# A hybrid encoder trunk on one Trainium2 core: softmax weights are transposed undivided, and each head pair's output is divided by the sums afterwards

## The chip, the cores and the metric

The kernel runs on one core of one Trainium2 chip. The metric is the device time of one launch in microseconds (us), and less is better. The core has a matrix engine (TensorE, PE in the profile, with its weight loads shown apart as PEld), a vector engine (VectorE, DVE), an activation engine (ScalarE, ACT), a general engine (GpSimd, POOL) and a queue for transfers (SyncE, SP). Each takes its own instructions in the order in which the built program lists them, and waits where a semaphore tells it to.

## What is computed

Two layers, each with a Fourier group and an attention group side by side, then a convolutional feed-forward part:

```python
for l in range(DEPTH):                              # 2
    h = rmsnorm(x, norm1[l]);  p = h @ w_in[l]      # x: 512 x 1024
    y_f = fourier_mix(u, w_fourier[l], b_fourier[l])   # 512 columns
    q, k = rope(rmsnorm(q)), rope(rmsnorm(k))       # 8 heads of q, 2 of k and v
    y_a = windowed_gqa(q, k, v, sink[l])            # |i - j| <= 128
    x = x + concat(rmsnorm(y_f), rmsnorm(y_a)) @ w_o[l]
    h = rmsnorm(x, norm2[l])
    x = x + (silu(gate) * val) @ w_down[l]          # gate, val = dwconv3(h @ w_up)
```

In `windowed_gqa` a softmax runs over a query's masked scores and one more logit, the head's learned sink; the sink's weight is then dropped, so it only adds to the sum that the other weights are divided by:

```python
probs = softmax(concat([scores, sink_col], axis=-1), axis=-1)[..., :-1]
out = einsum("bnkgqj,bnjkd->bnqkgd", probs, vb)
```

## The kernel before

Activations are kept transposed: channels on the 128 partitions, the 512 positions along the free axis, in four blocks of 128. Each float32 product runs as three passes over operands that are split into a high and a low part (`mm3`, L102 to L107; `split`, L93 to L100: ACT writes the high part, DVE subtracts to get the low one). The whole program is unrolled. A list scheduler with a timeline model orders the instructions of each engine when the program is built, starting from the order in which the code issues them. Tiles come from pools with a fixed number of buffers to a tag: the tag `tF` has 6 buffers of 128x512, `tA` has 6, and in PSUM `tp` has 2 banks, `sc` 2, `av` 1 and `mm` 3 (L70 to L72).

One layer runs in these stages: norm statistics and q, k, v products (L266 to L286); folding of h for the Fourier half (L289 to L300); `prep`, `turn_q` and `turn_k`, which normalise, rotate, split and transpose q and k (L312 to L368); the first Fourier products (L426 to L442); attention by head pairs (`attention`, L376 to L416, called for pair 3 and then 0, 1, 2); two Fourier stages (L466 to L497); the Fourier group's own output product, in four column tiles j (L501 to L529), its norm and split (L530 to L536); the output projection `proj` (L541 to L549) first for the Fourier half (`ys`, 32 groups of three matmuls) and then for the attention half (`ya`, 32 groups); then the feed-forward part (L569 to L626), which takes most of the time.

Attention works on 32 pieces to a layer (8 heads, 4 query blocks each), here called blocks. For one block: two score matmuls into an `sc` bank (L390); DVE adds the mask and takes the row's smallest negated score against the sink, `nmax` (L394); ACT takes the exponential in place over the scores and one column more, which POOL had filled with the negated sink (L393), so that the accumulated sum `den` has the sink in it (L397); DVE inverts it (L398); POOL multiplies the weights by it (L399); PE transposes two or three 128x128 tiles into a `tp` bank (L402); ACT and DVE split them into `pT` (L405). After four blocks, the products with the values go to `py` in the one `av` bank (L412). After two heads, `py` is split with the gain (L415) and its square added to `accA` (L416).

Two things set the order around the change. `steps` collects the last transpose of each block (L403), and the matmuls of the Fourier half of the projection may not be issued on PE before the block `STEP0 + n` with `STEP0 = 12` (L546), so that they can stand between the blocks of the later pairs. And the Fourier tiles j take their evicted product `u`, their output `y` and, from j = 1, a square from the tag `tF` (L522, L524, L528), as do several other steps, but not `attention`.

Of the kernel before, what the change touches and what calls it, by code (L numbers as in the profile page):

```python
# [8 lines left out]
F32 = mybir.dt.float32  # L9
# [7 lines left out]
P = 128  # L17
# [20 lines left out]
def encoder_kernel(tc, t):  # L38
    """Residual stream kept transposed (channels on partitions, positions free).

    Every float32 product runs as three float32r passes over exact splits
    a = hi + lo:  hi*hi + lo*hi + hi*lo.  RMSNorm's per-position factor is
    applied after the product it precedes where that is possible, its gain before.
    """
# [24 lines left out]
    # ---------------------------------------------------------------- helpers  # L69
# [23 lines left out]
    def split(hi, lo, src, scale=None, eng=None):  # L93
        """hi + lo = src * scale; hi has float32r's mantissa, lo the rest."""
# [7 lines left out]
    def mm3(out, a, b, start, stop, after=None, **kw):  # L102
        """out (+)= a^T b over split operands a = (hi, lo), b = (hi, lo)."""
# [28 lines left out]
    def rsqrt(ssq, n, inv, tag, bufs=2):  # L132
        """(ssq * inv + EPS) ** -0.5 on [P, n]: bit estimate and Newton steps."""
# [11 lines left out]
    def col_rstd(acc, inv, tag="tp"):  # L145
        """rstd per position as columns [position in block, block]."""
# [5 lines left out]
    def row_rstd(r, tag="tp"):  # L152
        """The same factors along the free axis, on every partition."""
# [7 lines left out]
    # -------------------------------------------------------------- constants  # L161
# [27 lines left out]
    # first use of the activation tables and of the tensor engine while the inputs arrive  # L189
# [33 lines left out]
    # ---------------------------------------------------------- norm of x tile  # L223
# [8 lines left out]
    def norm_tile(k, g, acc):  # L232
        """Split x[k] * gain and add x[k]^2 to acc."""
# [8 lines left out]
    def fold(dst, src, eng):  # L242
        """src[..., 512] -> 0..256 even part, 257..511 odd part of 1..255."""
# [4 lines left out]
    def load_wu(l, kk):  # L248
        """Two row tiles of W_in's Fourier columns, folded."""
# [14 lines left out]
    for l in range(L):  # L264
        # ----------------------------------------- norm statistics, q, k, v
# [22 lines left out]
        # -------------------------------------- folded h for the Fourier half  # L288
# [13 lines left out]
        # ------------------- QK-norm, RoPE, transposed split q (pairs) and k  # L302
# [9 lines left out]
        def prep(us):  # L312
            """Normalised, rotated and split rows of the units us (head pairs, or "k")."""
# [34 lines left out]
        def turn_q(qs, tag):  # L348
            """[hi; lo] of the pair's two heads, transposed."""
# [23 lines left out]
        steps = []  # L373
        ya = {}

        def attention(p, first_pair):  # L376
            g = p // 2
            py = psum("av")
            first = True
# [335 lines left out]
```

## Time and profile before

| | before |
|---|---|
| median of 3 runs | 1119.74 us (1118.82 to 1119.9) |
| span of the profiled execution, first to last instruction | 1114.8 us |
| median less span (launch and end, outside the span) | 4.9 us |
| PE busy | 1067.8 us, 96% of the span |
| DVE, ACT, POOL busy | 789.6, 523.5 and 329.5 us |
| mean granted TensorE clock | 0.986 of full speed |

A time of the profiled execution other than its span is not listed, so the span stands for it, and the 4.9 us beside it is taken as fixed. In the profile's rows a group is a line, an engine, an operation and its tiles, with a count, busy time and mean duration; in the timeline a row is a start, a duration and how many instructions were merged. A matmul's row lasts longer than the distance to the next one, since matmuls are pipelined: PE can be shown busy while its stream has gaps. A float32 matmul (L156) is counted as two instructions.

### The profile page before, as it was taken

What the parts mean: (1) busy time and instruction counts of PE and PEld (TensorE: products, weight loads), DVE (VectorE), ACT (ScalarE), POOL (GpSimd) and SP (SyncE); (2) the same over time, 40 slices, a digit from 0 to 9 for tenths busy, and PEclk for the clock granted to TensorE, in tenths of its full rate; (3) what the DMA queues carried; (4) which work ended last, traced back from release to release, by engine and by line L of the source; (5) the groups of instructions that cost most, each with busy time, mean ns of one, the idle gap of its engine ahead of it and who ended that gap; (6) DMA issues with size and microseconds to landing.
All of it is one profiled execution on the core that took longest, in us unless ns stands there. A gap on an engine that the chain in (4) does not pass through costs nothing.

```text
span 1114.8 us, 14505 instructions
## 1 busy us (share of the span) xinstructions
PE 1067.8 (96%) x5187; PEld 894.0 (80%) x5187; DVE 789.6 (71%) x1362; ACT 523.5 (47%) x964; POOL 329.5 (30%) x370
## 2 busy tenths in 40 slices
PE   7878899999999999999997999999999999999998
PEld 6767788788888888888896878878888888888887
DVE  8998874888773377785549978477887535787732
ACT  4537763465442244543434677445554323554421
POOL 5778655311010001024207865561111000010100
PEclk9979999999999999999999999999999999999999
DMA  6312112223323323224321310223332322323241
GB/s 218 109 57 95 39 39 76 91 85 95 108 78 92 114 95 95 95 83 135 114 85 59 94 39 1 76 61 109 95 95 83 104 94 98 105 88 110 78 129 59
DMA packets 33226, 99.66 MB, mean 89 GB/s; under 512 B 3705, under 2 KB 8066, under 8 KB 33154
## 3 DMA queue, kind: packets, MB, share of 16 engines
q1 hardware_dynamic: 33154, 98.74, 28.1%
q8 instruction: 41, 0.67, 0.2%
q14 instruction: 31, 0.25, 0.1%
HBM read 96.63 MB, written 2.10 MB: 89 GB/s over the span
## 4 chain that ended last, share of the span: by engine, by line
PE 79%; DVE 14%; issue 2%; POOL 2%; ACT 1%; DMA 1%; SPq 0%; DVEq 0%; POOLq 0%; ACTq 0%
PE ps L107 25%; PE ps L105 25%; PE ps L106 25%; DVE wlo L88 3%; DVE act L91 2%; DVE act L88 2%; DVE tF L91 1%; PE ps L402 1%; DVE tA L394 1%; DVE slab L88 1%; DVE tF L88 1%; PE ps L390 1%; DVE pT L88 1%; POOL tA L88 1%; PE ps L149 1%
## 5 line engine op out<-in xcount | busy, mean ns | idle before, releaser
L85 ACT ACTIVATE whi<-wraw 128x512 fp32r<-128x512 f32 (+1 forms) x336 | 205.4, 613 | 378.6 <-PE ps L107 341.7
L88 DVE TENSOR_TENSOR wlo<-wraw,whi 128x512 fp32r<-128x512 f32 (+1 forms) x304 | 256.0, 844 | 138.3 <-ACT whi L85 136.4
L107 PE MATMUL ps<-act,whi 128*128 128x512 f32 x768 | 299.9, 391 | 4.4 <-DVE act L91 4.4
L106 PE MATMUL ps<-act,wlo 128*128 128x512 f32 x768 | 300.0, 391 | 0.0
L105 PE MATMUL ps<-act,whi 128*128 128x512 f32 x768 | 299.8, 390 | 0.0
L88 POOL TENSOR_TENSOR tF<-tF,tF 128x512 f32<-128x512 f32 x44 | 58.1, 1321 | 523.0 <-DVE tF L91 479.7
L107 PEld LDWEIGHTS ps<-act,whi 128*128 128x128 f32 x768 | 144.7, 188 | 35.9 <-DVE act L91 6.4
L105 PEld LDWEIGHTS ps<-act,whi 128*128 128x128 f32 x768 | 144.6, 188 | 30.3
L106 PEld LDWEIGHTS ps<-act,wlo 128*128 128x128 f32 x768 | 144.7, 188 | 30.0
L91 DVE SCALAR_TENSOR_TENSOR tF<-tF,pb,tF 128x511 f32<-128x511 f32 x176 | 134.0, 766 | 11.2 <-ACT tF L85 8.6
L88 DVE TENSOR_TENSOR tF<-ps,rb 128x512 f32<-128x512 f32 x104 | 70.7, 688 | 76.4 <-PE ps L107 62.0
L105 PE MATMUL ps<-slab,whi 128*128 128x512 f32 (+2 forms) x228 | 87.9, 386 | 1.3 <-ACT slab L85 1.3
L106 PE MATMUL ps<-slab,wlo 128*128 128x512 f32 (+2 forms) x228 | 85.2, 374 | 0.0
L107 PE MATMUL ps<-slab,whi 128*128 128x512 f32 (+2 forms) x228 | 84.9, 375 | 0.1
L85 ACT ACTIVATE tF<-tF,pb 128x512 f32<-128x512 f32 x88 | 71.6, 816 | 13.5 <-DVE tF L88 7.1
L88 POOL TENSOR_TENSOR wlo<-wraw,whi 128x512 fp32r<-128x512 f32 x40 | 55.1, 1379 | 47.0 <-ACT whi L85 42.7
L88 DVE TENSOR_TENSOR x<-x,ps 128x512 f32<-128x512 f32 (+1 forms) x49 | 33.0, 675 | 40.2 <-PE ps L107 40.2
L88 POOL TENSOR_TENSOR acc<-acc,sq 128x512 f32<-128x512 f32 x28 | 41.3, 1477 | 49.8 <-ACT sq L85 48.9
L106 PE MATMUL ps<-pT,wlo 128*128 128x512 f32 (+1 forms) x132 | 51.0, 386 | 0.0
L107 PE MATMUL ps<-pT,whi 128*128 128x512 f32 (+1 forms) x132 | 50.9, 385 | 0.0
L105 PE MATMUL ps<-pT,whi 128*128 128x512 f32 (+1 forms) x132 | 50.8, 385 | 0.0
L105 PEld LDWEIGHTS ps<-slab,whi 128*128 128x128 f32 x228 | 42.9, 188 | 9.1 <-ACT slab L85 1.8
(166 smaller groups left out, 1797.4 us busy)
## 6 DMA issues: line engine op xcount, KB each, us to landing
wraw<-in_w_up_dram SPq DMA_DIRECT2D x88, 512.0 KB, 3.6
wraw<-in_w_down_dram SPq DMA_DIRECT2D x32, 512.0 KB, 3.5
wraw<-in_w_o_dram SPq DMA_DIRECT2D x16, 512.0 KB, 3.6
wraw<-in_w_qkv_dram SPq DMA_DIRECT2D x16, 384.0 KB, 3.5
wraw<-in_w_down_dram SPq DMA_DIRECT2D x32, 192.0 KB, 2.4
wraw<-in_w_in_dram SPq DMA_DIRECT2D x8, 512.0 KB, 4.5
wraw<-in_w_fold_dram SPq DMA_DIRECT2D x8, 512.0 KB, 3.5
x<-in_xT_dram SPq DMA_DIRECT2D x8, 256.0 KB, 6.2
```

The lines of the kernel that those rows point to most:

```text
L85: return nc.scalar.activation(out, in_, func, **kw)
L88: return (eng or nc.vector).tensor_tensor(out, a, b, op=op)
L91: return nc.vector.scalar_tensor_tensor(out=out, in0=a, scalar=s, in1=b, op0=op0, op1=op1)
L105: nc.tensor.matmul(out, a[0], b[0], start=start, stop=False, **kw)
L106: nc.tensor.matmul(out, a[1], b[0], start=False, stop=False, **kw)
L107: nc.tensor.matmul(out, a[0], b[1], start=False, stop=stop, **kw)
L149: nc.tensor.matmul(pt[:, 2 * b:2 * b + 2], acc[:, b * P:(b + 1) * P], ones2, start=True, stop=True)
L390: nc.tensor.matmul(sc[:, :n], qT[p][:, e, i * P:(i + 1) * P], kT[g][:, s, j0 * P:(j1 + 1) * P], start=s == 0, stop=s == 1)
L394: nc.vector.tensor_tensor_reduce(out=pr[:, :n], in0=sc[:, :n], in1=mask[:, m0:m0 + n], scale=-1.0 / math.sqrt(HD), scalar=nsink[:, l, h:h ...
L402: tr = nc.tensor.transpose(pp[:, j * P:(j + 1) * P], pr[:, j * P:(j + 1) * P], ident)
```

## The change

Four things change in `attention`. The exponential runs over the scores alone, with no sink column, and the transposed weights are undivided: POOL's fill, DVE's reciprocal and POOL's multiplication for each block go. Once per head, ACT takes the exponential of `nmax + sink`, DVE adds it to the four sums and inverts them. Once per head pair, ACT spreads the inverted sums over a 128x512 tile, four float32 matmuls with the identity transpose it into a `tp` bank, ACT copies that to a tile `y`, and DVE multiplies `py` by it. The split and the square then read `y` instead of `py`. The two new tiles of each pair come from the tag `tF`.

```diff
+            den = sp.tile([P, 2, NB], F32, tag="den", name=nm("den"), bufs=2)
...
-                    pr = temp(385, "tA")
-                    nc.gpsimd.tensor_copy(pr[:, n:n + 1], nsink[:, l, h:h + 1])
+                    pr = temp(384, "tA")
...
-                    act(pr[:, :n + 1], pr[:, :n + 1], AF.Exp, scale=-1.0, bias=nmax[:, i:i + 1], accum_out=den[:, i:i + 1])
-                    nc.vector.reciprocal(den[:, i:i + 1], den[:, i:i + 1])
-                    nc.gpsimd.tensor_scalar(pr[:, :n], pr[:, :n], den[:, i:i + 1], 1.0, op0=ALU.mult, op1=ALU.mult)
+                    act(pr[:, :n], pr[:, :n], AF.Exp, scale=-1.0, bias=nmax[:, i:i + 1], accum_out=den[:, e, i:i + 1])
...
+                es = sp.tile([P, NB], F32, tag="es", name=nm("es"), bufs=2)
+                act(es, nmax, AF.Exp, bias=sink[:, l, h:h + 1])
+                tt(den[:, e], den[:, e], es, ALU.add)
+                nc.vector.reciprocal(den[:, e], den[:, e])
...
+            wide = temp(512, "tF").rearrange("p (b e d) -> p b e d", b=NB, e=2)
+            act(wide, den.rearrange("p e b -> p b e")[:, :, :, None].to_broadcast([P, NB, 2, HD]))
+            pd = psum("tp")
+            for i in range(NB):
+                nc.tensor.matmul(pd[:, i * P:(i + 1) * P], wide[:, i].rearrange("p e d -> p (e d)"), ident,
+                                 start=True, stop=True)
+            y = temp(512, "tF")
+            act(y, pd)
+            tt(y, py, y, ALU.mult)
             ya[p] = pair("act")
-            split(ya[p][:, 0, :], ya[p][:, 1, :], py, scale=gA[:, l, p:p + 1])
-            add_square(accA, py, first_pair, nc.vector if p == 2 else nc.gpsimd)
+            split(ya[p][:, 0, :], ya[p][:, 1, :], y, scale=gA[:, l, p:p + 1])
+            add_square(accA, y, first_pair, nc.vector if p == 2 else nc.gpsimd)
```

The scheduler's order changes with it. On ACT in layer 0 the evictions of the Fourier output tiles j (`tF` from a `ps` bank with `pa`, 128x258) stood among the exponentials (`tA`) of the first head pairs:

```order
L85 ACTIVATE tF_1713<-ps_1682,pa 128x258
L85 ACTIVATE wt_1726<-wtr_1724 1x128
L85 ACTIVATE tA_1032,den_1027<-tA_1032,nmax_1026 128x257
L85 ACTIVATE tA_1046,den_1027<-tA_1046,nmax_1026 128x385
L85 ACTIVATE act_939<-ps_940 128x512
L85 ACTIVATE act_939<-ps_946 128x512
L85 ACTIVATE whi_1890<-wraw_1884 128x512
L85 ACTIVATE whi_1924<-wraw_1922 128x512
L85 ACTIVATE accF_1681<-tF_1715 128x512
L85 ACTIVATE tF_1751<-ps_1720,pa 128x258
```

Now the first two of them (`tF_1685`, `tF_1723`) come right behind the last pair's new tiles (`tF_1518`, the spread sums, and `tF_1525`, their transposed copy), and the other two follow:

```order
L85 ACTIVATE tF_1518<-den_1389 128x512
L85 ACTIVATE pT_1455<-ps_1462 128x256
L85 ACTIVATE pT_1455<-ps_1473 128x384
L85 ACTIVATE pT_1455<-ps_1485 128x384
L85 ACTIVATE pT_1455<-ps_1497 128x256
L85 ACTIVATE tF_1525<-ps_1520 128x512
L85 ACTIVATE tF_1685<-ps_1654,pa 128x258
L85 ACTIVATE tF_1723<-ps_1692,pa 128x258
L85 ACTIVATE act_1528<-tF_1525,pa 128x512
L85 ACTIVATE sq_1531<-tF_1525 128x512
```

So all four Fourier evictions of the layer moved from the beginning of the attention to behind its end. On PE in layer 0, matmuls of the Fourier half of the projection (`slab` by `whi` or `wlo`, 128x512) stood between the transposes (L402) of the later pairs:

```order
L402 MATMUL ps_1436<-ident,tA_1430 128x128 x3
L105 MATMUL ps_1946<-slab_1873,whi_1928 128x512
L106 MATMUL ps_1946<-slab_1873,wlo_1929 128x512
L107 MATMUL ps_1946<-slab_1873,whi_1928 128x512
L402 MATMUL ps_1451<-ident,tA_1445 128x128 x3
L105 MATMUL ps_1946<-slab_1877,whi_1928 128x512
L106 MATMUL ps_1946<-slab_1877,wlo_1929 128x512
L107 MATMUL ps_1946<-slab_1877,whi_1928 128x512
L402 MATMUL ps_1466<-ident,tA_1460 128x128 x2
```

Now the stretch of the last head of the last pair holds attention alone (products with the values, `pT` by `vz`, and the new float32 matmuls, L421), and the Fourier output tile j = 1 (`slab` by `whi`, 128x256) comes behind the last product with the values:

```order
L107 MATMUL ps_1388<-pT_1455,vz_120 128x256
L105 MATMUL ps_1388<-pT_1455,vz_120 128x384
L106 MATMUL ps_1388<-pT_1455,vz_121 128x384
L107 MATMUL ps_1388<-pT_1455,vz_120 128x384
L421 MATMUL ps_1520<-ident,tF_1518 128x128 x4
L105 MATMUL ps_1388<-pT_1455,vz_120 128x384
L106 MATMUL ps_1388<-pT_1455,vz_121 128x384
L107 MATMUL ps_1388<-pT_1455,vz_120 128x384
L105 MATMUL ps_1388<-pT_1455,vz_120 128x256
L106 MATMUL ps_1388<-pT_1455,vz_121 128x256
L107 MATMUL ps_1388<-pT_1455,vz_120 128x256
L105 MATMUL ps_1693<-slab_1640,whi_1704 128x256
```

A little further on PE, once the last Fourier tile is through, both norm factors are made (L149 sums the squares, L156 spreads the factors), and only behind them begins the Fourier half of the projection:

```order
L149 MATMUL ps_1812<-ones_116,accF_1653 128x2 x4
L156 MATMUL ps_1833<-ident,nr_1818 128x128 x4
L156 MATMUL ps_2029<-ident,nr_2014 128x128 x4
L105 MATMUL ps_1866<-slab_1841,whi_1858 128x512
L106 MATMUL ps_1866<-slab_1841,wlo_1859 128x512
L105 MATMUL ps_1880<-slab_1841,whi_1862 128x512
L106 MATMUL ps_1880<-slab_1841,wlo_1863 128x512
```

All 32 groups of `ys` now stand behind the attention in one piece, with the 32 of `ya` behind them. Layer 1 is moved in the same way.

More of the change, by code (lines that the diff above doesn't have):

```diff
@@ L379, in attention @@
             first = True
+            den = sp.tile([P, 2, NB], F32, tag="den", name=nm("den"), bufs=2)
             for e in range(2):
                 h = 2 * p + e
-                nmax, den = [sp.tile([P, NB], F32, tag=z, name=nm(z), bufs=3) for z in ("nmax", "den")]
+                nmax = sp.tile([P, NB], F32, tag="nmax", name=nm("nmax"), bufs=3)
                 pT = temp(2560, "pT", F32R).rearrange("p (s b q) -> p s b q", s=2, q=P)
```

## The prediction

> **What bounds the kernel now.** I read the page first, then the table by stretches of 5 us, then the timeline, then the groups of instructions by form.
>
> ```profile
> PE 1067.8 (96%) x5187; PEld 894.0 (80%) x5187; DVE 789.6 (71%) x1362; ACT 523.5 (47%) x964; POOL 329.5 (30%) x370
> ```
>
> PE is the bound, and POOL, which loses most of the work here, is the emptiest engine. What counts is whether PE's stream through the attention gets longer. The stretches of attention in layer 1, the ends of both projections, and one matmul behind such an end:
>
> ```profile
> 665.00:670.00 5.00, 4.58 (x29) 3.68 (x30) 4.93 (x16) 3.95 (x11) 4.44 (x9) 1.00 0.02 5
> 680.00:685.00 5.00, 4.66 (x35) 4.16 (x33) 4.62 (x19) 4.46 (x13) 2.78 (x9) 1.00 0.00 0
> 710.00:715.00 5.00, 5.00 (x27) 4.26 (x26) 2.09 (x4) 1.56 (x3) 1.29 (x1) 1.00 0.09 20
> 200.00:205.00 5.00, 3.00 (x13) 1.95 (x12) 5.00 (x7) 1.03 (x3) 2.88 (x2) 1.00 0.24 98
> 205.00:210.00 5.00, 5.00 (x16) 3.98 (x17) 5.00 (x7) 2.68 (x5) 1.84 (x2) 0.66 0.37 107
> 750.00:755.00 5.00, 5.00 (x24) 4.14 (x23) 5.00 (x7) 2.34 (x5) 2.24 (x2) 1.00 0.32 105
> ```
>
> The columns are PE, PEld, DVE, ACT and POOL busy, the granted clock, and the transfers. At 665 to 685 attention runs nearly alone: PE is shown 92% to 93% busy (4.58 and 4.66 of 5), but matmul rows overlap the next one, so its stream has gaps, and DVE, ACT and PE are all loaded. At 710 projection groups fill what attention leaves. In this program the Fourier half of the projection is what covers attention's waits, and the orders printed above show that the change takes that cover away.
>
> Next, where one layer's attention and Fourier projection begin and end: the first transposes and the last `ys` matmul of layer 0, the same two of layer 1, and two rows twelve matmuls apart in a dense stretch.
>
> ```profile
> 109.87 0.77 PE L402 MATMUL ps<-ident,tA 128*128 128x128 f32 x5
> 176.05 0.40 PE L107 MATMUL ps<-slab,whi 128*128 128x512 f32 x1
> ...
> 656.36 0.77 PE L402 MATMUL ps<-ident,tA 128*128 128x128 f32 x5
> 720.66 0.40 PE L107 MATMUL ps<-slab,whi 128*128 128x512 f32 x1
> ...
> 197.70 0.39 PE L107 MATMUL ps<-act,whi 128*128 128x512 f32 x1
> 200.42 0.39 PE L107 MATMUL ps<-act,whi 128*128 128x512 f32 x1
> ```
>
> From first transpose to last `ys` it takes 176.45 - 109.87 = 66.6 us in layer 0 and 721.06 - 656.36 = 64.7 us in layer 1. Dense matmuls come every (200.42 - 197.70) / 12 = 0.227 us, so the 32 groups of `ys` are 96 x 0.227 = 21.8 us of PE in each.
>
> **The change, part by part.** What is removed:
>
> ```profile
> L393 POOL COPY tA<-nsink 128x1 f32<-128x1 f32 x64 | 20.2, 321 | 15.4 <-PE ps L402 10.7 <-DVE wlo L88 4.3
> L399 POOL TENSOR_SCALAR tA<-tA,den 128x384 f32<-128x384 f32 x32 | 19.3, 603 | 12.9 <-DVE den L398 12.8
> L399 POOL TENSOR_SCALAR tA<-tA,den 128x256 f32<-128x256 f32 x32 | 18.1, 572 | 6.2 <-DVE den L398 6.2
> L398 DVE RECIPROCAL den<-den 128x1 f32<-128x1 f32 x64 | 9.1, 151 | 1.8 <-ACT tA L85 1.6
> ```
>
> POOL loses 20.2 + 19.3 + 18.1 = 57.6 us, which it had to spare. DVE loses 9.1 us and gets 32 small operations (half of them sums, half inversions) at about the same 0.151 us, 4.8 us, and eight multiplications. For each block, 0.15 + 0.6 us of latency between exponential and transpose goes. Scores run up to six blocks ahead in `tA`, so that latency is worth something only where a block is waited for.
>
> What is added on PE is eight sets of four float32 matmuls; the nearest row is the one that spreads a norm factor, of the same four shapes:
>
> ```profile
> 133.85 1.06 PE L156 MATMUL ps<-ident,nr 128*128 128x128 f32 x8
> 724.11 0.95 PE L149 MATMUL ps<-ones,acc 128*128 128x2 f32 x8
> ```
>
> That is 1.06 us a pair, 4.2 us a layer, on PE's path. Now attention without cover. First by the pace that it had nearly alone:
>
> ```profile
> 665.93 0.49 PE L402 MATMUL ps<-ident,tA 128*128 128x128 f32 x3
> 684.35 0.41 PE L402 MATMUL ps<-ident,tA 128*128 128x128 f32 x2 [0.34 <-DVE pT L88]
> ```
>
> Between these two rows lie 14 blocks: 18.42 / 14 = 1.32 us a block. Inside lie a norm's L149 and L156 (0.95 + 1.06 us, 0.14 a block), which leave; the new PE work (1.06 / 8 = 0.13) comes. So about 1.31, and 32 blocks take 42 us. Second, by ACT, the engine with the most new work there:
>
> ```profile
> L85 ACT ACTIVATE tA<-tA,nmax 128x385 f32<-128x385 f32 x32 | 19.6, 612 | 5.1 <-DVE den L398 1.7 <-POOL tA L393 1.3 <-DVE nmax L394 0.5
> L85 ACT ACTIVATE tA<-tA,nmax 128x257 f32<-128x257 f32 x32 | 16.2, 506 | 2.1 <-DVE den L398 1.5 <-POOL tA L393 0.4
> L85 ACT ACTIVATE pT<-ps 128x384 fp32r<-128x384 f32 x32 | 15.3, 484 | 8.1 <-PE ps L402 7.8
> L85 ACT ACTIVATION_READ_ACCUMULATOR tA<-tA,nmax 128x1 f32 x64 | 12.1, 190 | 0.0
> L85 ACT ACTIVATE pT<-ps 128x256 fp32r<-128x256 f32 x32 | 12.0, 376 | 6.9 <-PE ps L402 6.6
> L85 ACT ACTIVATE act<-ps,pa 128x512 fp32r<-128x512 f32 x8 | 5.5, 682 | 3.3 <-PE ps L107 3.0
> L85 ACT ACTIVATE rb<-ps 128x512 f32<-128x512 f32 x8 | 4.8, 600 | 8.5 <-PE ps L156 8.5
> L85 ACT ACTIVATE sq<-ps 128x512 f32<-128x512 f32 x6 | 3.6, 597 | 1.6 <-DVE act L91 1.6
> ```
>
> A pair of heads has four exponentials and four `pT` copies of each size, eight reads of the sums, a split, a square, and now two 128x512 copies (priced as `rb`, 0.600) and two 128x4 exponentials (nearest rows 0.190 and 0.376; I take 0.25): 4 x (0.612 + 0.506 + 0.484 + 0.376) + 8 x 0.190 + 0.682 + 0.597 + 1.2 + 0.5 = 12.4 us. Two rows show that a following instruction starts 0.09 us before the end of the one before (0.49 + 106.17 against 106.57):
>
> ```profile
> 106.17 0.49 ACT L85 ACTIVATE tA<-tA,nmax 128x257 f32<-128x257 f32 x1
> 106.57 0.19 ACT L85 ACTIVATION_READ_ACCUMULATOR tA<-tA,nmax 128x1 f32 x1
> ```
>
> Over 30 instructions that takes off 2.7, so ACT needs 9.7 us a pair, 38.8 a layer, without any wait. At each pair's end ACT's split of `y` waits for DVE's multiplication, which waits for the last product with the values, and the transposes of the next pair queue behind that on PE, since the next pair's first product needs the one `av` bank: a microsecond or so a pair. 38.8 + 4 = 43. The two ways agree; I take 42 us, between 38 (no waits) and 48 (1.5 us a block).
>
> Behind the attention comes a chain that lay under it before: the evictions of the four Fourier tiles, their assembly on DVE, squares on ACT, sums on POOL, L149, two inverse square roots on DVE, L156, its copy, the scaling, the split. Its prices:
>
> ```profile
> L85 ACT ACTIVATE slab<-tF 128x512 fp32r<-128x512 f32 x40 | 24.7, 631 | 23.3 <-POOL tF L88 15.7 <-PE ps L107 3.8 <-DVE tF L244 2.5
> L88 POOL TENSOR_TENSOR accF<-accF,tF 128x512 f32<-128x512 f32 x6 | 7.7, 1282 | 0.1
> L91 DVE SCALAR_TENSOR_TENSOR tF<-tF,pa,rb 128x512 f32<-128x512 f32 x8 | 5.6, 759 | 0.0
> L85 ACT ACTIVATE tF<-ps,pa 128x258 f32<-128x258 f32 x8 | 3.8, 473 | 2.1 <-PE ps L107 1.8
> L88 DVE TENSOR_TENSOR slab<-tF,slab 128x512 fp32r<-128x512 f32 x40 | 30.4, 778 | 0.0
> L85 ACT ACTIVATE wt<-wtr 1x128 fp32r<-1x128 f32 x8 | 2.4, 295 | 0.8 <-DMA wtr<-in_w_fourier_dram 0.8
> ```
>
> In the new order ACT has 14 instructions from the last product to the square of j = 3 (three evictions at 0.473, nine of 128x512 at about 0.62 by the rows of such, two small ones at 0.295): 7.6 us, with waits for DVE's assembly about 9. Then 1.28 on POOL, 0.95 for L149, two sets of twelve dependent small DVE operations, interleaved (24 x 0.16, an estimate from the 0.151 of L398, 4 us), 1.06 for L156, and 0.600 + 0.759 + 0.631 to the first split: 9.3. The low parts come behind all four scalings, 4 x 0.759 + 0.778 after the copy, about a microsecond more than PE's six ready matmuls cover. That is 19 to 20 us; PE has the rest of the Fourier tiles inside it and stands still for some 4 us at the inverse square roots. After the 2.0 us of PE's wait inside 200 to 205 the granted clock was 0.66 for the next 5 us, which costs 1.7; in 750 to 755, after an equal wait, it was 1.00. I take 20 us for the chain, 16 to 25 with both ends of this.
>
> The Trainium skill ("TensorE: Matmul & The Clock Gate", Part 1) says that the clock returns to half after an idle window of about 3.4 us and to full after as long a busy one. By that rule the standstill costs each layer about 1.7 us, and the chain would be nearer to 22; the row of 0.66 agrees, that of 1.00 shows that a 2 us wait need not do it.
>
> The sum for a layer, from first transpose to last `ys`: 1.5 us of Fourier matmuls of j = 0 and 1 that still stand between (estimate: 13 at about 0.12), 42, 20, and 21.8 for `ys` now dense: 85.3, against 66.6 and 64.7. Behind it, the attention half's L149 and L156 (2.0 us), which stood among the `ya` groups, now lie in the chain, so 2.0 comes off. Layer 0: +16.7, layer 1: +18.6, together +35.3 us. The rest of a layer is unchanged: the wait at the end of `ya` is for DVE, whose work there is the same. The profiled span would be 1150.1 us, and 1119.74 + 35.3 = **1155 us** against the median.
>
> **The rivals.** First, faster: the block's latency is what held attention, so that without POOL and the inversions it runs at PE's own pace. Two products with the values in a dense stretch:
>
> ```profile
> 131.09 0.33 PE L105 MATMUL ps<-pT,vz 128*128 128x384 f32 x1
> 131.26 0.34 PE L106 MATMUL ps<-pT,vz 128*128 128x384 f32 x1
> ```
>
> They start 0.17 us apart for 384 columns, 0.12 in proportion for 256. A block has two score matmuls and, on the mean, three products, 5 x 0.145, and 2.5 transposes at 0.11 (the first row above, 0.77 us for five, less one row's length), and 0.13 of new work: 1.13 us, with a quarter of the scores ahead 34 us a layer. The chain would overlap the last pair down to its bare 9.3 and some 2 of evictions: 1.5 + 34 + 11 + 21.8 - 2.0 = 66.3, against 66.6 and 64.7, so +1.3 us; and if the projection's end loses its 2.0 us wait in each layer and the slow clock behind it (1.7), the kernel takes 1115 us. It decides where attention and chain together fall under some 44 us. Against it: ACT alone needs 38.8. Chance 0.03.
>
> Second, hidden: ACT's train for the Fourier tiles overlaps the attention's tail, and blocks come at 1.15 us, so a layer pays 37 + 14 in place of 42 + 20: 11 us less in each, 1133 us. For it speaks the missing POOL step; against it that ACT's evictions stand behind the last pair's copy. Chance 0.10.
>
> Third, the clock: attention with gaps runs at half clock, PE's 34 us become 68 in place of 42, and the kernel takes 1155 + 2 x 26 = 1207 us. The stretches at 665 and 680 had such gaps at 1.00. The Trainium skill (same page, Part 4) says that transposes don't count as busy for the clock gate; by that rule the attention, a quarter of it transposes and uncovered, could fall to half. The rows so far don't show it. Chance 0.05.
>
> Fourth, no change: the order printed isn't what bounds, and the cover is replaced by the feed-forward part's first groups, 1119 to 1122 us. PE's order rules that out unless my reading is wrong. Chance 0.02.
>
> **How the numbers follow.** My forecast has 0.80. Its own bounds are 38 + 16 (8 us less a layer, 1139) and 48 + 25 (11 us more a layer, 1177); the range goes down to the second rival, from 1133 to 1177, and leaves out the others. About 2.2 us (0.2%) is what a measurement of this kernel can tell from no change. Faster 0.03, same 0.02, slower 0.95.
>
> **What would show it.** In the profile after: transposes in an unbroken series at 1.2 to 1.5 us a block; 60 us or so from first transpose to first `ys`; PE waiting 3 to 5 us at L156 for the small DVE operations; POOL's L393 and L399 gone without any shorter span. Wrong would be `ys` matmuls between transposes, under 1.1 us a block, or a chain under 14 us.

## The result, and the profile after

| | before | after |
|---|---|---|
| median of 4 runs | 1119.28 us (1116.16 to 1119.9) | 1161.22 us (1160.82 to 1163.52) |
| ratio, 95% interval | | 1.0386 (1.037 to 1.0402) |
| span of the profiled run | 1114.8 us | 1159.4 us |
| mean granted clock of TensorE | 0.986 | 0.971 |

The forecast was 1155 us, with 1133 to 1177 as its range. The change makes the kernel 3.9% slower. By the medians it costs 41.9 us, by the two spans 44.6. The changed kernel's profiled execution took 1161.1 us, 1.7 more than its span; the 4.9 us between median and span that the table of the kernel before shows are therefore not a fixed cost of a launch, and its profiled execution was one of its faster ones.

The page's totals for the changed kernel:

```profile
PE 1094.0 (94%) x5251; PEld 914.0 (79%) x5251; DVE 797.0 (69%) x1338; ACT 535.4 (46%) x996; POOL 281.1 (24%) x242
```

POOL lost 329.5 - 281.1 = 48.4 us of work, and nothing came of it. PE is busy 26.2 us longer and the span is 44.6 us longer, so PE waits more. Not all of the 26.2 is new work: the 64 instructions more are the eight sets of divisor matmuls, 8.4 us by their rows below, and the granted clock fell. Over the span that is (1 - 0.971) x 1159.4 - (1 - 0.986) x 1114.8 = 18 us of full clock lost, an upper limit for its share in the loss, since PE also stood still in part of that time. Now PE's timeline of the changed kernel at the places that bound its attention: first transpose, last product with the values, the statistics and the spreading of the two norms, first and last `ys` matmul of layer 0; then the same without the norms in layer 1. The columns are start, duration, instruction and shapes; in brackets the wait ahead of it and its releaser.

```profile
108.02 1.03 PE L401 MATMUL ps<-ident,tA 128*128 128x128 f32 x5
155.59 0.28 PE L107 MATMUL ps<-pT,vz 128*128 128x256 f32 x1
160.54 1.05 PE L149 MATMUL ps<-ones,acc 128*128 128x2 f32 x8 [0.30 <-DVE acc L88]
168.49 1.66 PE L149 MATMUL ps<-ones,accF 128*128 128x2 f32 x7 [5.26 <-POOL accF L88]
172.88 3.75 PE L156 MATMUL ps<-ident,nr 128*128 128x128 f32 x16 [2.52 <-DVE nr L91]
177.06 0.80 PE L105 MATMUL ps<-slab,whi 128*128 128x512 f32 x1 [0.43 <-ACT slab L85]
200.12 0.39 PE L107 MATMUL ps<-slab,whi 128*128 128x512 f32 x1
...
675.49 0.44 PE L401 MATMUL ps<-ident,tA 128*128 128x128 f32 x2
724.85 0.28 PE L107 MATMUL ps<-pT,vz 128*128 128x256 f32 x1
746.38 0.80 PE L105 MATMUL ps<-slab,whi 128*128 128x512 f32 x1 [0.43 <-ACT slab L85]
769.79 0.40 PE L107 MATMUL ps<-slab,whi 128*128 128x512 f32 x1
```

In the kernel before, the first `ys` matmul of layer 0 was this row:

```profile
138.51 0.50 PE L105 MATMUL ps<-slab,whi 128*128 128x512 f32 x1 [0.98 <-ACT slab L85]
```

It stood 28.6 us behind the first transpose, in the middle of the attention; now it stands 69.0 us behind it, and every `ys` matmul comes after everything of the attention. The whole stretch, from first transpose to the end of the last `ys`, is 200.51 - 108.02 = 92.5 us in layer 0 (66.6 before) and 770.19 - 675.49 = 94.7 us in layer 1 (64.7 before). Cut into the prediction's pieces, layer 0 and layer 1: attention 155.87 - 108.02 = 47.9 and 49.6 us, chain to the first `ys` 21.2 and 21.3 us, `ys` 23.4 and 23.8 us.

The same time in stretches of 5 us (PE, PEld, DVE, ACT, POOL busy, then the granted clock):

```profile
130.00:135.00 5.00, 4.41 (x32) 3.89 (x31) 3.25 (x11) 3.69 (x9) 0.29 (x1) 1.00 0.00 0
145.00:150.00 5.00, 2.70 (x17) 1.62 (x14) 4.84 (x12) 4.25 (x12) 1.27 (x1) 1.00 0.02 5
165.00:170.00 5.00, 1.51 (x7) 1.51 (x8) 1.31 (x3) 0.74 (x2) 3.12 (x3) 0.50 0.36 105
170.00:175.00 5.00, 2.48 (x12) 2.42 (x13) 2.41 (x24) 0.04 (x1) 0.00 (x0) 0.50 0.00 0
175.00:180.00 5.00, 4.57 (x18) 3.70 (x18) 4.40 (x7) 3.24 (x6) 0.00 (x0) 0.67 0.00 0
```

The first two lie in the attention: PE has gaps (4.41 and 2.70 of 5) and nothing fills them. The next two lie in the chain: no engine is loaded, each waits for the one before it, and the clock is at half. In the last one the first `ys` run, and over its 5 us the clock is still at 0.67.

Part of the loss comes back behind the last `ys`. The one wait of PE there, and the 165th `act` matmul behind the last `ys`, in layer 0; first before, then after:

```profile
204.82 0.50 PE L107 MATMUL ps<-act,whi 128*128 128x512 f32 x1 [2.00 <-DVE act L91]
220.45 0.39 PE L107 MATMUL ps<-act,whi 128*128 128x512 f32 x1
```

```profile
229.09 0.50 PE L107 MATMUL ps<-act,whi 128*128 128x512 f32 x1 [0.21 <-DVE act L91]
239.04 0.39 PE L107 MATMUL ps<-act,whi 128*128 128x512 f32 x1
```

From the start of the last `ys` (176.05 before, 200.12 after) to this matmul it is 44.40 us before and 38.92 after: 5.5 us less, and in layer 1 43.53 against 38.96, 4.6 less. The 2.00 us wait became 0.21. The books: the first transpose comes 1.9 us earlier (109.87 to 108.02), layer 0 costs 25.9 - 5.5 = 20.4, layer 1 30.0 - 4.6 = 25.4; together 44.0 of the 44.6 us.

### The profile page after: what moved, and what is told of

Same layout as the page of the kernel before. It is cut to its first block, busy times and chain, and to the rows that moved or that the text cites. A ratio compares the mean times of both kernels' runs of the same rounds, so it can differ in the third digit from the quotient of the medians.

```text
span 1159.4 us, 14412 instructions
## 1 busy us (share of the span) xinstructions
PE 1094.0 (94%) x5251; PEld 914.0 (79%) x5251; DVE 797.0 (69%) x1338; ACT 535.4 (46%) x996; POOL 281.1 (24%) x242
## 4 chain that ended last, share of the span: by engine, by line
PE 79%; DVE 13%; issue 2%; POOL 2%; ACT 2%; DMA 1%; SPq 0%; DVEq 0%; ACTq 0%; POOLq 0%
PE ps L105 25%; PE ps L107 25%; PE ps L106 24%; DVE wlo L88 2%; PE ps L392 2%; DVE act L91 2%; DVE act L88 1%; DVE tF L88 1%; PE ps L401 1%; DVE tA L395 1%; DVE tF L91 1%; PE ps L421 1%; PE ps L149 1%; DVE pT L88 1%; PE ps L156 1%
## 5 line engine op out<-in xcount | busy, mean ns | idle before, releaser
L88 DVE TENSOR_TENSOR wlo<-wraw,whi 128x512 fp32r<-128x512 f32 (+1 forms) x304 | 252.2, 831 | 138.4 <-ACT whi L85 136.6
L106 PEld LDWEIGHTS ps<-act,wlo 128*128 128x128 f32 x768 | 144.2, 188 | 30.1
```

The source lines that it names most:

```text
L88: return (eng or nc.vector).tensor_tensor(out, a, b, op=op)
L106: nc.tensor.matmul(out, a[1], b[0], start=False, stop=False, **kw)
```

## The experiments

Theory: the time was lost because the new tiles `wide` and `y` take their buffers from the tag of the Fourier output tiles, so that the Fourier half's last tiles, its norm and all `ys` stand behind the attention. Rival: the new operations cost it (divisor matmuls on PE, copies on ScalarE, a longer chain at a pair's end). The runs were taken on three chips, on which the kernel before took 1118.5, 1118.9 and 1118.4 us; each ratio is against the kernel before on the same chip. The values of one kernel spread over 2 to 4 us, so a difference of about 2 us between two medians of four or five values is not clear of noise.

### Another buffer tag, the arithmetic of the change kept

```diff
-            wide = temp(512, "tF").rearrange("p (b e d) -> p b e d", b=NB, e=2)
+            wide = temp(512, "sq").rearrange("p (b e d) -> p b e d", b=NB, e=2)
...
-            y = temp(512, "tF")
+            y = temp(512, "sq")
```

> The changed kernel with one word altered twice: `wide` and `y` are taken from tag sq (2 buffers, unused in this stage by the Fourier half) instead of tF. All the arithmetic of the change stays. Lost-cover theory: the ys groups stand between the transposes again, so first transpose to last ys comes back from 92.5 us to about 67 to 72 us in layer 0, and the run takes 1117 to 1128 us: 1119.3 as before, plus at most 8 pairs of 1.05 us for the four divisor matmuls (8.4 us) if none of them falls into a gap of TensorE. Rival, the new operations themselves cost the time (divisor matmuls, two more copies per pair on ScalarE, one more product on VectorE): nothing of them is removed, so the run stays at 1155 to 1163 us.

Measured: 1129.5 us, 1.0094 (1.0079 to 1.011) of before. First transpose, first and last `ys` of its layer 0:

```profile
108.08 0.77 PE L401 MATMUL ps<-ident,tA 128*128 128x128 f32 x5
140.02 0.50 PE L105 MATMUL ps<-slab,whi 128*128 128x512 f32 x1
180.93 0.40 PE L107 MATMUL ps<-slab,whi 128*128 128x512 f32 x1
```

The first `ys` is back inside the attention, 31.9 us behind the first transpose, and the stretch is 73.3 us, a little over the 67 to 72 expected. Two words in the source give back 1161.2 - 1129.5 = 31.7 us with all of the change's operations in place. So the lost cover is shown as the main cause. What stays is 11 us, 1.5 above the upper end of the forecast for this run; the sections on the removal and on the divisor matmuls say what it is made of.

### The same tag, the calls moved

The two statements that call the attention move behind the loop over the Fourier output tiles:

```diff
-        attention(3, True)
-        for p in range(3):
-            attention(p, False)
...
             yf.append(y)
+        attention(3, True)
+        for p in range(3):
+            attention(p, False)
         rbF = row_rstd(col_rstd(accF, 1.0 / FW, "mm"), "mm")
```

> The changed kernel with `wide` and `y` still from tag tF, but the two statements that call the attention stand behind the loop that makes the four Fourier output tiles instead of ahead of it. Lost-cover theory, in the form that buffers of one tag are given out in the order of the program: the Fourier tiles get their buffers first, the cover is back, and the run takes 1117 to 1130 us, as with the other tag. Rival, the tiles of the tag are simply too few (6 buffers for both uses at once): the pairs' tiles now wait for the Fourier tiles or the reverse, and the time stays above 1140 us. Rival, the new operations cost the time: 1155 to 1163 us.

Measured: 1131.1 us, 1.0112 (1.0096 to 1.0127), 1.1 above the range of the theory. Its first `ys` matmul of layer 0 stands 31.7 us behind the first transpose (108.72), inside the attention again:

```profile
140.42 0.43 PE L105 MATMUL ps<-slab,whi 128*128 128x512 f32 x1
```

Same tag, same six buffers, same operations; only who asks for a buffer first is different, and 30.1 us come back. The number of buffers wasn't the trouble but the order in which the program hands them out: a Fourier tile that asks behind the last pair waits until that pair has given a buffer back. Moved calls also give the scheduler another starting order; the run with the other tag, which keeps the calls in place, is the one that singles out the buffers.

### The old arithmetic with two tiles of that tag

```diff
+            wide = temp(512, "tF")
+            act(wide, py)
+            y = temp(512, "tF")
+            nc.vector.tensor_copy(y, wide)
             ya[p] = pair("act")
-            split(ya[p][:, 0, :], ya[p][:, 1, :], py, scale=gA[:, l, p:p + 1])
-            add_square(accA, py, first_pair, nc.vector if p == 2 else nc.gpsimd)
+            split(ya[p][:, 0, :], ya[p][:, 1, :], y, scale=gA[:, l, p:p + 1])
+            add_square(accA, y, first_pair, nc.vector if p == 2 else nc.gpsimd)
```

> The kernel before, with its division on GpSimd kept and none of the change's arithmetic, but with two tiles of tag tF per pair as the change has them: ScalarE copies the pair's output into the first, VectorE copies that into the second, and the split and the square read the second. Lost-cover theory: all ys groups stand behind the attention, and the run takes 1142 to 1162 us. The lower end is for an attention without cover of 42 us per layer as predicted (+20.4 in the stage, -7 at the end of the ya groups, twice), the upper for 48 us as the changed kernel shows. Rival, the change's own operations cost the time: only two copies per pair are added here, 16 of about half a microsecond, so 1119 to 1127 us.

Measured: 1146.1 us, 1.0244 (1.023 to 1.0258). The loss appears with none of the new arithmetic in the kernel, which shows the cause from the other side. The run also gives what no other one has, an attention without cover and without the new work. PE's time from first transpose to last product in both layers, with its busy time (the columns as above), of this kernel and then of the changed one:

```profile
110.65:152.45 41.80, 37.18 (x225) 29.59 (x224) 33.45 (x117) 32.15 (x94) 22.56 (x55) 1.00 0.05 14
669.26:710.54 41.28, 37.43 (x225) 29.50 (x224) 33.42 (x117) 32.26 (x95) 20.89 (x54) 1.00 0.05 14
```

```profile
108.02:155.87 47.85, 42.36 (x269) 35.10 (x268) 34.54 (x106) 38.02 (x110) 3.82 (x3) 1.00 0.04 12
675.49:725.13 49.64, 44.01 (x272) 37.01 (x271) 33.95 (x107) 37.73 (x109) 3.81 (x3) 0.97 0.04 12
```

Without the new work the attention takes 41.8 and 41.3 us, with POOL's multiplication and all; with it 47.9 and 49.6. PE's busy time grows by 5.2 and 6.6 us, of which the divisors are 4.2 and a dozen matmuls of the Fourier tiles, which the other run hasn't got there, much of the rest, and its time without work stays between 3.9 and 5.6 us in all four. That fits a PE whose added work lengthens the attention. It doesn't show it, since ACT's busy time grows too, from 32 to 38 us.

### The removal alone

The changed kernel without `es`, the reciprocals, `wide`, the divisor matmuls, `y` and the product:

```diff
-                es = sp.tile([P, NB], F32, tag="es", name=nm("es"), bufs=2)
-                act(es, nmax, AF.Exp, bias=sink[:, l, h:h + 1])
-                tt(den[:, e], den[:, e], es, ALU.add)
-                nc.vector.reciprocal(den[:, e], den[:, e])
...
-            split(ya[p][:, 0, :], ya[p][:, 1, :], y, scale=gA[:, l, p:p + 1])
+            split(ya[p][:, 0, :], ya[p][:, 1, :], py, scale=gA[:, l, p:p + 1])
```

> Half of the change alone: the weights are transposed undivided and nothing takes the division's place, so the sums, the sink's share and the division are left out of the computation. What remains removed: 32 small copies and 32 multiplications on GpSimd and 32 reciprocals on VectorE per layer. The cover stays. Lost-cover theory with TensorE bound in this stage: between 1112 and 1120 us, the gain being at most what TensorE waits there now (some 2 to 4 us per layer). Rival, the chain from scores to transpose sets the pace of the covered stage: every block is shorter by about a microsecond on GpSimd and a small VectorE step, 32 blocks, and the run falls to 1090 to 1108 us.

Measured: 1121.4 us, 1.0021 (1.0012 to 1.003): not faster, just slower than before, and above the ranges of both forecasts. With 49.5 us of POOL's work (329.5 to 280.0) and all 64 reciprocals gone, and nothing in their place, nothing is won. The rival that the block's latency holds the covered attention falls. Why it even loses a little is taken up below.

### What the divisor matmuls cost

Three kernels start from the one with tag `sq` (1129.5 us).

```diff
-                nc.tensor.matmul(pd[:, i * P:(i + 1) * P], wide[:, i].rearrange("p e d -> p (e d)"), ident,
-                                 start=True, stop=True)
+                nc.tensor.transpose(pd[:, i * P:(i + 1) * P], wide[:, i].rearrange("p e d -> p (e d)"), ident)
```

> The kernel with `wide` and `y` from tag sq (1129.5 us), with the four divisor matmuls of a pair issued as transposes of the same tile, which give the same values. Four transposes of 128x128 are 0.65 us in this case's rows, four such matmuls 1.05 us. Theory, what is left of the change's cost beside the cover is TensorE's own time in those matmuls: 8 pairs x 0.40 = 3.2 us less, about 1126. Rival, what is left is the longer chain at a pair's end (sums, reciprocal, two ScalarE copies, product) that holds the pair's output bank: no change, 1128.5 to 1130.5 us.

```diff
-            pd = psum("tp")
-            for i in range(NB):
-                nc.tensor.matmul(pd[:, i * P:(i + 1) * P], wide[:, i].rearrange("p e d -> p (e d)"), ident,
-                                 start=True, stop=True)
...
-            act(y, pd)
+            act(y, wide.rearrange("p b e d -> p (b e d)"))
```

> The same kernel (tag sq) without the divisor matmuls: ScalarE's second copy reads the first instead of their bank, so the outputs are not divided by the right sums; every other instruction and the chain at a pair's end stay. Theory, TensorE's own time: 8 x 1.05 = 8.4 us less than 1129.5, that is 1119 to 1122.5 us, the same as the removal alone (1121.4). Rival, the chain at the pair's end: at most the matmuls' own latency goes, 1126 to 1130 us.

```diff
                 nc.tensor.matmul(pd[:, i * P:(i + 1) * P], wide[:, i].rearrange("p e d -> p (e d)"), ident,
                                  start=True, stop=True)
+                nc.tensor.matmul(pd[:, i * P:(i + 1) * P], wide[:, i].rearrange("p e d -> p (e d)"), ident,
+                                 start=True, stop=True)
```

> The kernel with tag sq, with every divisor matmul issued twice into the same place, so the values stay. Theory, TensorE's own time: 8 x 1.05 = 8.4 us more than 1129.5, that is 1136.5 to 1139.5 us. Rival, the matmuls stand in gaps of TensorE: 1129 to 1132 us.

Measured: none 1122.7 us, as transposes 1127.2, as matmuls 1129.5, twice 1137.7. One set in the kernel with tag `sq`, and one in the kernel with transposes:

```profile
138.45 1.05 PE L421 MATMUL ps<-ident,sq 128*128 128x128 f32 x8
```

```profile
137.97 0.60 PE L421 MATMUL ps<-ident,sq 128*128 128x128 f32 x4
```

Eight sets of 1.05 us are 8.4 us: doubling them cost 8.2, leaving them out gave 6.8. Eight times 0.45 us less would be 3.6; transposes gave 2.3, a time between the two forecasts of that run and not clear of noise alone. The doubled and the missing sets decide: the time goes with PE's own work, in a stage that is covered again, and the gaps of PE take in little of it. The longer chain at a pair's end has almost no price: without the matmuls, but with both copies, the product and the sums, the kernel takes 1122.7 us against 1121.4 for the removal alone, 1.3 us that are within the noise. So the 11 us that tag `sq` leaves are 6.8 for the divisor matmuls, 1.3 for all the rest of the new work, and 2.9 that the removal alone loses.

### The changed kernel without the divisor matmuls

```diff
-            pd = psum("tp")
-            for i in range(NB):
-                nc.tensor.matmul(pd[:, i * P:(i + 1) * P], wide[:, i].rearrange("p e d -> p (e d)"), ident,
-                                 start=True, stop=True)
             y = temp(512, "tF")
-            act(y, pd)
+            act(y, wide.rearrange("p b e d -> p (b e d)"))
```

> The changed kernel, tiles from tag tF as it has them, without the divisor matmuls in the same way (outputs not divided by the right sums). The attention has no cover here. Theory: TensorE sets the pace there too, so the first transpose to the last product falls from 47.9 and 49.6 us to 42 to 44 us per layer, and the run from 1161 to 1147 to 1153 us. Rival, the longer chains set the pace and the matmuls stand in its gaps, as the prediction had it: the attention stays at 46 to 50 us, and the run at 1157 to 1162 us.

Measured: 1140.4 us, below the lower end of both. Its last product and first `ys` of layer 0:

```profile
154.87 0.27 PE L107 MATMUL ps<-pT,vz 128*128 128x256 f32 x1
168.39 0.80 PE L105 MATMUL ps<-slab,whi 128*128 128x512 f32 x1 [0.43 <-ACT slab L85]
```

Taking the matmuls out also moved the rest of the Fourier tile j = 1 and the tiles 2 and 3 to ahead of the last products, so the chain shrank from 21.2 to 13.2 us and the attention, with them inside, to 46.1. Two things changed at once, and the run doesn't measure the pace of the attention. An estimate: the 36 matmuls that moved follow each other there at 0.12 us, 4.3 us in all, so without them the attention would take about 41.8. That is 6.1 us less than 47.9, where the divisors' rows are 4.2, so in an attention without cover they may cost more than their own length. The run does show what the short chain of the prediction's second rival would have looked like.

### Why the removal alone loses two microseconds

In the removal's trace, just ahead of layer 1's attention, PE waits for the splits of the Fourier half's first stage. That wait in the kernel before, and in the removal alone:

```profile
632.04 0.39 PE L105 MATMUL ps<-th,slab 128*128 128x258 f32 x1 [0.90 <-DVE slab L91]
```

```profile
634.60 0.39 PE L105 MATMUL ps<-th,slab 128*128 128x258 f32 x1 [3.76 <-DVE slab L91]
```

With other work gone, the scheduler put VectorE's three products of raw q ahead of the splits:

```profile
631.32 2.89 DVE L88 TENSOR_TENSOR act<-pT,qk3r 128x512 f32<-128x512 f32 x3
```

The same wait, 3.75 to 3.83 us, stands in layer 1 of the four kernels with tag `sq` above, so it drops out of the differences between them. The changed kernel hasn't got it, so the 31.7 us that tag `sq` gave back are the lost cover less what this wait takes. The loss of the removal lies in layer 1: by PE's rows the last `ys` of layer 0 starts 1.2 us earlier than in the kernel before (174.83, 176.05), and from there to the last `ys` of layer 1 it is 4.2 us longer (548.8, 544.6). Two stretches that follow, in the same order, before and then the removal alone:

```profile
635.00:640.00 5.00, 3.93 (x30) 2.99 (x29) 5.00 (x12) 4.64 (x12) 5.00 (x6) 1.00 0.57 198
640.00:645.00 5.00, 4.32 (x27) 3.29 (x26) 5.00 (x12) 3.59 (x10) 5.00 (x5) 1.00 0.00 1
```

```profile
635.00:640.00 5.00, 4.69 (x19) 3.68 (x18) 5.00 (x10) 2.79 (x9) 5.00 (x5) 0.59 0.19 41
640.00:645.00 5.00, 4.61 (x19) 3.31 (x20) 5.00 (x14) 3.21 (x9) 1.53 (x2) 0.50 0.16 66
```

Three kernels force the splits first, in the removal, in the kernel before, and in the change with all mends. The code of the splits is also moved ahead of the call of the attention (not shown), so the scheduler starts from another order in both layers:

```diff
-        for p, qs in enumerate(prep((0, 1, 2))):
+        for p, qs in enumerate(prep((0, 1, 2), last[-1])):
...
-                tt(t1, qraw[u], r[:, i, :, :, None].to_broadcast(shape), ALU.mult)
+                with tc.issue_after(after) if after is not None else nullcontext():
+                    tt(t1, qraw[u], r[:, i, :, :, None].to_broadcast(shape), ALU.mult)
```

> The removal alone (weights transposed undivided, division and the sink's share left out; 1121.4 us, 2.3 to 2.9 over before) with one order changed at a layer's start: VectorE's three products of raw q with its inverse roots wait until the Fourier half's first stage has been split, so the splits come first, and the code that makes them stands ahead. In the removal's trace TensorE stands 3.76 us there in layer 1 behind these products (2.89 us), 0.90 us in the kernel before, and its clock is at 0.50 to 0.59 of full speed for the next 10 us, at 1.00 before. Theory, the removal's small loss is this accident of order: 1116.5 to 1119.5 us. Rival, the loss comes from elsewhere, or the next wait takes its place: 1120.5 to 1123 us or more.

> The kernel before, with the same order forced at each layer's start and nothing else. The order there had the splits before the products already in layer 1, with a wait of TensorE of 0.90 us. Theory of the accident: 1116.5 to 1119.5 us, nothing or at most a microsecond per layer won. Rival, the q products are needed early by the attention's first scores: 1120 to 1124 us.

> The change with all mends together: tiles from tag sq, divisors as transposes (1127.2 us), and the splits ahead of the q products. Theory: the transposes' 8 x 0.65 = 5.2 us over what the removal with this order takes, that is 1122 to 1125 us, still slower than before, since TensorE's added work has nothing to be paid with. Rival, the removed work of GpSimd and VectorE is worth something once the order is mended: below 1118 us.

Measured: the removal 1115.1 us, 0.9972 (0.9962 to 0.9982); the kernel before 1124.5, 1.005 (1.0037 to 1.0062); the mended change 1123.4, 1.0042 (1.0028 to 1.0055). The longest wait of PE for these splits in layer 1, in the removal with the forced order, and the stretch of 5 us behind it:

```profile
637.24 0.38 PE L105 MATMUL ps<-th,slab 128*128 128x256 f32 x1 [1.47 <-DVE slab L91]
```

```profile
640.00:645.00 5.00, 3.81 (x25) 2.57 (x23) 5.00 (x13) 3.28 (x9) 1.13 (x1) 1.00 0.00 0
```

The same two in the kernel before with the forced order:

```profile
641.15 0.58 PE L105 MATMUL ps<-th,slab 128*128 128x256 f32 x1 [2.66 <-DVE slab L91]
```

```profile
645.00:650.00 5.00, 5.00 (x18) 3.64 (x17) 4.07 (x12) 1.10 (x3) 1.58 (x3) 0.50 0.00 0
```

In the removal the long wait and the half clock behind it are gone, and the run is 6.3 us shorter, more than the loss that was to be explained and below the range of the theory. Not all of it can be the wait: of the 6.1 us between the two spans (1117.7 and 1111.6), 2.2 are won by the last `ys` of layer 0 (174.83, 172.66), where the removal's longest wait for such splits is 1.46 us, and 4.0 from there to the last `ys` of layer 1. So the accident in layer 1, its wait and its clock, can account for 4.0 us at most; the rest came with the new order, and no run here shows its cause.

In the kernel before, the forced order costs 6 us. The products now wait for the last split of the first stage and stand ahead of the next stage's splits instead:

```profile
637.17 3.59 DVE L88 TENSOR_TENSOR act<-pT,qk3r 128x512 f32<-128x512 f32 x3
```

PE's wait of 2.66 us ends 0.4 us behind them, and the clock falls there. That is what the theory calls an accident of order, in another place; the rival's time came about (1124.5 against 1120 to 1124), but no wait of the first scores is shown. This order is no general gain. The mended change lies in the range that the theory gave, 3.5 us above the removal with its 8 sets of transposes (1115.1 + 8 x 0.6 = 1119.9), and no run here explains the 3.5. None of the versions that compute the reference beats the kernel before. The most that a free division could win in the orders tried here is the removal's 3.3 us, and each set of divisors on PE takes 0.6 to 1.05 us of it, eight times.

## Why the prediction was right, step by step

**The cover.** Right, and shown from three sides: another tag gives the time back, another order of calls gives it back with the same tag, and the tag alone costs it with the old arithmetic. Two of the signs named for it came as well: transposes in an unbroken series, and no shorter span for POOL's lost work. The other two came out of size: from first transpose to first `ys` it was 69.0 and 70.9 us where 60 or so was written, and PE waited 2.52 us at L156 where 3 to 5 were. A block took 1.50 and 1.55 us, at the upper edge of the 1.2 to 1.5.

**Attention, 42 us with 1.5 us of Fourier matmuls.** Mis-sized, and the largest error: 47.9 and 49.6 in place of 43.5. The 1.31 us a block came from a stretch of the covered attention, with a norm's matmuls (0.14) exchanged for the divisors (0.13). The run with the old arithmetic has 41.8 and 41.3 us over 32 blocks, 1.31 and 1.29 without any divisor. So the divisors' 4.2 us a layer were not paid for by the norm that left; that exchange is the term that was mis-sized. The sum of that run's 41.8 and 41.3, 4.2 for the divisors and the 1.5 of Fourier matmuls is 47.5 and 47.0. In layer 1 the clock takes some of the rest: two stretches at the attention's end,

```profile
715.00:720.00 5.00, 3.87 (x16) 3.11 (x17) 3.04 (x7) 2.93 (x9) 1.28 (x1) 0.76 0.01 2
720.00:725.00 5.00, 4.67 (x31) 4.14 (x29) 1.83 (x4) 1.98 (x5) 0.00 (x0) 0.90 0.00 0
```

lose 5 x 0.24 + 5 x 0.10 = 1.7 us. About 0.9 us there stays without a name. The sum itself is not exact: the old arithmetic has POOL's step and its latency in it, the new one hasn't. That the two ways of pricing agreed (42 and 43) was no proof: one took a norm's matmuls out of PE's stream, the other didn't count PE's work at all. ACT's work was priced well, at 38.8 us against 38.0 and 37.7 busy; ACT did not set the pace alone.

**The chain, 20 us.** Measured 21.2 and 21.3. The standstill of some 4 us was put at the inverse square roots; there it is 2.52, and the longer wait, 5.26 and 4.49 us, is for POOL's sum `accF`; the row of layer 1:

```profile
737.80 1.87 PE L149 MATMUL ps<-ones,accF 128*128 128x2 f32 x8 [4.49 <-POOL accF L88]
```

In layer 0 it is 12.6 us from the last product to the end of that wait, where 10.3 (9 and POOL's 1.28) were put, and 8.6 from there to the first `ys`, about the 9 that were put. The Trainium skill ("TensorE: Matmul & The Clock Gate", Part 1) has the clock at half after an idle window of about 3.4 us; by that rule the chain was to be nearer to 22. The trace agrees on the half clock, which was 0.50 from 165 to 175, and the chain came out between 20 and 22. It doesn't agree on the idle window: PE's wait of 5.26 us goes from 163.23 to 168.49, and the clock fell in the second of these stretches. At half for (1 - 0.81) / 0.5 = 0.4 us of it, it fell about 1.4 us into the wait.

```profile
163.00:164.00 1.00, 0.23 (x2) 0.02 (x1) 0.76 (x3) 0.71 (x2) 0.00 (x0) 1.00 0.00 0
164.00:165.00 1.00, 0.00 (x0) 0.00 (x0) 0.31 (x1) 1.00 (x3) 0.63 (x1) 0.81 0.00 1
```

For the same reason the row of 0.66, which the prediction took as agreeing, agrees only in how long the clock stayed down (0.34 of 5 us lost, 3.4 us at half); the wait ahead of it was 2.00 us.

**`ys`, 21.8 us.** Measured 23.4 and 23.8. Of the difference 0.4 is the length of the last matmul's row, which 96 starts leave out. The first 3 us ran in the stretch at 0.67; the prediction had counted the slow clock only inside the chain.

**Behind `ys`, -2.0 us.** Measured -5.5 and -4.6. The step that failed here is "the wait at the end of `ya` is for DVE, whose work there is the same". The work is the same, but it starts earlier. The factor of the attention's norm, which every eviction of `ya` needs, was spread 11.7 us behind the start of the last `ys` in the kernel before, in this row; now it is spread at 172.88, ahead of the first.

```profile
187.71 1.05 PE L156 MATMUL ps<-ident,nr 128*128 128x128 f32 x8
```

DVE in the 15 us behind the last `ys`, before and after:

```profile
176.45:191.45 15.00, 15.00 (x75) 12.61 (x75) 5.16 (x17) 3.67 (x6) 6.42 (x6) 1.00 0.34 106
```

```profile
200.50:215.50 15.00, 15.00 (x68) 12.40 (x67) 8.67 (x10) 7.49 (x12) 12.55 (x9) 1.00 0.36 107
```

DVE does 8.67 us there in place of 5.16, and the 2.00 us wait with its slow clock is gone. Of the 5.5 us, 1.9 are the two norm steps that left (the first 96 `act` matmuls behind the last `ys` take 21.80 us in place of 23.69), as forecast; the rest is that wait and clock. The run with the old arithmetic and the lost cover has the same (38.94 us to the 165th matmul), those with the cover back don't (43.58 in the kernel with tag `sq`): it belongs to the order, not to the arithmetic.

So two errors of opposite sign, 4.4 and 6.1 us too little in the attention, 3.5 and 2.6 too little gain behind it, partly cancelled, with 1.2 and 1.6 to 2.0 us too little for chain and `ys`. The forecast of +35.3 us fell 6.6 short of the medians and 9.3 short of the spans; without the gain behind `ys` that it hadn't seen, it would have been some 15 short of the spans, so a part of its nearness is luck.

**The rivals.** PE's own pace: refuted, since attention and chain together took 69.0 us, where it needed them under some 44, and the attention alone 47.9, where it put 34. A hidden chain: not so in the changed kernel, 21.2 us, but without the divisors it became 13.2. Half clock through the attention: refuted, since the clock was 1.00 over the attention of layer 0 and 0.97 over that of layer 1, where only the last 10 us had 0.76 and 0.90. The Trainium skill (same page, Part 4) doesn't count transposes as busy for the clock; no run here sets them apart from the matmuls around them, and an attention without cover, in which 80 of PE's 269 recorded matmuls are transposes, held 1.00 for 47.85 us. No change: refuted.

## What to carry to other kernels

Before taking a temporary from a shared set of buffers, see who asks next for one in program order: two tiles that are small in bytes can put another stage, and all that it covers, behind the stage that borrows them, and the printed order of the bounding engine shows it. Price new work on the engine that bounds at nearly its full duration, also where that engine shows gaps, and price removed work on an idle engine at nothing until a run with the removal alone says otherwise. A wait of the bounding engine can cost twice, once as the wait and once in the clock behind it.

## What the runs showed of the hardware

Four float32 matmuls of 128x128 by 128x128 take 1.05 us and are recorded as eight instructions; four transposes of the same tiles take 0.60 us and are recorded as four.

The clock was at 0.50 in the stretch behind a wait of 2.66 us, and at 0.59 and 0.50 behind one of 3.76; behind waits of 0.90 and 1.47 us it stayed at 1.00, and behind two nearly equal waits in the kernel before (2.00 and 1.99 us) it fell once and stayed once. It doesn't fall at a fixed point of the wait: in the changed kernel it fell about 1.4 us into a wait of 5.26, and behind the wait of 3.76, which ended at 634.60, only about 1.3 us after its end: from 635 to 636 it was still 0.97, from 636 to 637 it was 0.50. PE's idle time was shorter there than the time for which the clock then stayed down: it was still at half in the stretch from 640 to 645.
